# The samples' last 16 steps of gathered rows: from the stage of the weighted sums to behind the first half's last norm

## The chip, the cores and the metric

The kernel runs on one core of one Trainium2 chip. The metric is device time in microseconds (us) of one execution, the median over several runs. The profile is one execution on the same core, read by the hardware profiler. The engines are PE (TensorE, with PEld for its weight loads), DVE (VectorE), ACT (ScalarE), POOL (GpSimd) and SP (SyncE). Each takes its own instructions strictly in order.

## What is computed

One layer of a hybrid decoder for 512 prompt tokens and 32 sample tokens (8 sequences of 4), 544 columns in all, 1024 channels. Two token mixers come first; the change doesn't touch them. Then come a product-key expert layer and a gate, and the change lies where these two meet:

```python
def peer_ffn(h, ...):                # per token: 8 heads, 16 of 16384 experts each
    ...
    act = gelu(einsum('nd,nhkd->nhk', hb, expert_u[idx]))
    wgt = gate * act
    return einsum('nhk,nhkd->nd', wgt, expert_v[idx])

x = x + peer_ffn(rmsnorm(x, g_ffn), ...)
ple_gate = sigmoid(rmsnorm(x, g_ple) @ w_ple_gate)
x = x + (p @ w_ple) * ple_gate       # y = rmsnorm(x, g_final)
```

## The kernel before

**Tokens.** The first 384 prompt tokens (ND) go through the experts densely: all 16384 experts are computed in 128 blocks, masked by gates. The other 128 prompt tokens and the 32 sample tokens use gathered rows: a step is either a dot of a gathered row of expert_u with the token (`dot`, lines 1115 to 1117) or a gathered row of expert_v times its weight, added to an accumulator (`add`, lines 1122 to 1127). The prompt's 128 tokens have one token per partition and 128 picks, 256 steps. The 32 samples are laid four times over the 128 partitions, a quarter of the heads each, so 32 picks and 64 steps. `sides` hands out these 320 steps in order; the last 16 are adds of picks 16 to 31 of the samples. In front of the first of them stands one small product (line 1137) of 16 weights with their gates. The accumulators are `accs[0]` (prompt) and `accs[1]` (samples; the trace calls the tile accg).

**A gather** (line 1109) is an indirect DMA on POOL's queue of 128 rows of 1024 floats, 512 KB, into one of four buffers `rows` (NGR). A buffer is free again when the dot or add that read it is done.

**The stage of the weighted sums** (loop over j at line 1204 on) multiplies the 128 blocks' activations with expert_v on PE into three accumulators `pacc`, 36 matmuls of 512 columns for a block. The weights are float32 split in two parts: ACT copies the high part (line 123, whi), DVE subtracts to get the low part (line 124, wlo); three products stand for one. The loop takes three of the 320 steps per block. What is left is written out behind it (lines 1214, 1215). A scheduler places the instructions on each engine, so DVE's order isn't the order of the text.

**The last stage** begins with pacc: for three blocks of 128 tokens ACT copies pacc into `ot`, PE transposes it (line 1250), DVE adds it to x (line 1252, `residual`). Beside this the PLE input p is multiplied with w_ple on PE (line 1266, pw). Then the 544 columns are treated as two halves of 272 columns (HS). Half 0, the first half, holds prompt tokens only, all of them dense. Half 1, the second, holds the rest: dense tokens, the 128 tokens of accs[0] (`residual(3, ...)`) and the 32 samples, which a product with `sel` folds from four copies to one (line 1287, pts). The loop at lines 1277 to 1297 makes for each half the norm (`rms_rstd`: squares on ACT, line 98 and 101; sums sa on DVE, line 102; a product with ones; root on ACT with its table load, line 108; broadcast on PE, line 116), scales x (xn, line 1295) and splits it into fh and fl. The second loop, lines 1298 to 1314, makes for each half 8 chunks: a weight block of 512 KB is loaded and split, PE does 24 matmuls of 272 columns (line 1304, pj), ACT the sigmoid (sg, line 1306), DVE multiplies by pw and adds to x (lines 1307, 1308). Then come the final norm, its scaling (yo, line 1313) and the stores. The text calls the chunks 0 to 7 (half 0) and 8 to 15 (half 1). High and low parts of a weight block have two buffers, so the split for chunk c+2 waits for PE's end of chunk c.

`tc.issue_after(ins)` binds the instructions that are written in its block, those on the engine of `ins` alone, to come behind `ins` on that engine.

Of the kernel before, what the change touches and what calls it, by code (L numbers as in the profile page):

```python
# [14 lines left out]
OP = mybir.AluOpType  # L15
# [27 lines left out]
LATE = 110  # L43
XL, NYO = 118, 6
TW = 3, 2
NXN = 3
NRW, NHW = 3, 4
BACT = (4, 4, 4)
# [8 lines left out]
def step_kernel(ctx: ExitStack, tc: tile.TileContext, xT, pT, pk, wab, win, wbr, wout, wq, keysT, eu, eur, ev,  # L57
                wple, wpg, sh, sd, scv, yT, o_hp, o_dp, o_cv, o_hs, o_ds, gdram, ysp, gsp, x1s, asp, usp):
    nc = tc.nc
    V, S, G, PE = nc.vector, nc.scalar, nc.gpsimd, nc.tensor  # L60
# [9 lines left out]
    def par(name, i=0, n=1):  # L70
        return pkt[:, PK[name] + i:PK[name] + i + n]
# [50 lines left out]
    def split(hi, lo, src):  # L122
        S.activation(hi, src, AF.Copy)  # L123
        return V.tensor_sub(lo, src, hi.bitcast(F32))  # L124
# [3 lines left out]
    def wload(src, blocks=True):  # L128

        raw = wr.tile([128, 1024], F32, name="wraw", tag="wraw", bufs=NRAW)  # L130
        nc.sync.dma_start(raw, src)
        hi = wp.tile([128, 1024], F32R, name="whi", tag="whi", bufs=NHI)
        lo = wp.tile([128, 1024], F32R, name="wlo", tag="wlo", bufs=NHI)
        split(hi, lo, raw)
        if not blocks:
            return hi, lo
        return hi.rearrange("p (k c) -> p k c", c=128), lo.rearrange("p (k c) -> p k c", c=128)
# [55 lines left out]
    for hf in range(2):  # L193
        r0 = rms_rstd(sp_, pn0, lambda k: x0[:, k, HS[hf]], 8, hf)
        for k in range(8):
            xn = sp_.tile([128, HT], F32, name="xn", tag="xn", bufs=3)
# [580 lines left out]
    for h in range(NH):  # L777
# [4 lines left out]
        i = done = 0  # L782
# [90 lines left out]
    for i, hi, lo in ((0, hh, hl), (1, hh2, hl2)):  # L873
        if i:
            r1 = rms_rstd(x1p, pn1, lambda k: x1[:, k, HS[1]], 8, 1)
        for k in range(8):
            xn = hf[:, k] if i else qp.tile([128, HT], F32, name="xn", tag="xn", bufs=2)
# [106 lines left out]
    def ublock(j):  # L984
        ps = dots_u(*wload(eu[j]))
        i = slots.pop(0)
        acts[j] = act[:, i], i
        S.activation(act[:, i], ps[:, :ND], AF.Gelu_apprx_tanh)
# [152 lines left out]
    def sides():  # L1141
        yield from g_steps(0, htok, 128)
        yield from g_steps(1, hsam, 32)

    steps = sides()
    made = 0
# [21 lines left out]
    def prep(j):  # L1168

        wh = ep.tile([128, ND], F32R, name="wgh", tag="wgh", bufs=2)  # L1170
        wl = ep.tile([128, ND], F32R, name="wgl", tag="wgl", bufs=2)
        raw = wr.tile([128, 1024], F32, name="vraw", tag="wraw", bufs=NRAW)
        loads.append(nc.sync.dma_start(raw, ev[j]))
        if j >= NPRE and j % 4 == 0:
            ggs[0] = ggs.pop(j, None) or gates_in()
            nc.sync.dma_start(ggs[0], gdram[:, (j - NPRE) // 4])
        if j + 3 in spilled:
            reload(j + 3)
        a, i = acts.pop(j)
        if j >= NPRE:  # L1180
            V.tensor_mul(a.rearrange("p (c n) -> p c n", n=32), a.rearrange("p (c n) -> p c n", n=32), ggs[0][:, :, j % 4])
        gated.append(split(wh, wl, a))
        if i is not None:
            slots.append(i)
        vh = wp.tile([128, 1024], F32R, name="whi", tag="whi", bufs=NHI)
        vl = wp.tile([128, 1024], F32R, name="wlo", tag="wlo", bufs=NHI)
        split(vh, vl, raw)
        return wh, wl, vh, vl

    def products(j, wh, wl, vh, vl):  # L1190
        for i, (w_, v_) in enumerate(((wh, vh), (wl, vh), (wh, vl))):
            for t in range(3):
                ts = slice(t * 128, (t + 1) * 128)
                for hf in range(2):
                    PE.matmul(pacc[t][:, hf], w_[:, ts], v_[:, hf * 512:(hf + 1) * 512],  # L1195
                              start=(j == 0 and i == 0), stop=(j == 127 and i == 2))
# [6 lines left out]
    for j in range(128):  # L1203
        now = ready
        while late and len(acts_made) < nlate * (j + 1) / LATE:
            acts_made.append(late.pop(0))
            ublock(acts_made[-1])
        if j < 127:
            ready = prep(j + 1)
        products(j, *now)  # L1210
        with tc.issue_after(gated[min(HJ, j + 1)].ins) if j < HOLD else ExitStack():
            for _ in range(3):
                next(steps, None)
    for _ in steps:
        pass
    eps.close()
    wst.close()
    lts.close()
# [12 lines left out]
    def tile_(tag, bufs, shape, dt=F32):  # L1231
        return lp.tile(shape, dt, name=tag, tag=tag, bufs=bufs)

    yo0 = [tile_("yo", NYO, [128, 2, HT]) for _ in range(2)]
    tile_("xn3", NXN, [128, HT])
    tile_("sg2", 2, [128, HT])
    ph = tile_("fh", 2, [128, 2, T], F32R)
    pl = tile_("fl", 2, [128, 2, T], F32R)
    NRAW, NHI = TW
    wp = wr = tail.enter_context(tc.tile_pool(name="wpt", bufs=2, side="right", reuse_waits="tile"))  # L1240
# [6 lines left out]
    def residual(t, ot, k0):  # L1247
        p = psu.tile([128, 512], F32, name="pt", tag="pu").rearrange("p (a b) -> p a b", a=4)
        for k in range(4):
            PE.transpose(p[:, k], ot[:, k * 128:(k + 1) * 128], ident)  # L1250
        xc = x1[:, k0:k0 + 4, t * 128:(t + 1) * 128]
        V.tensor_add(xc, xc, p)
# [20 lines left out]
    def norm(i):  # L1273
        xs = x1[:, :, HS[i]]
        r = rms_rstd(x2p, pn.tile([128, 512], F32, name="pn", tag="pn").rearrange("p (a b) -> p a b", a=1),
                     lambda k: xs[:, k], 8, 0)
        return xs, r

    parts = []
    for i in range(2):  # L1280
        if i == 1:
            for k0 in range(0, 8, 4):
                residual(3, accs[0][:, k0 * 128:k0 * 128 + 512], k0)
            for k0 in range(0, 8, 4):
                p = psu.tile([128, 512], F32, name="pts", tag="pu")[:, :4 * NS].rearrange("p (a b) -> p a b", a=4)
                for k in range(4):
                    PE.matmul(p[:, k], accs[1][:, (k0 + k) * 128:(k0 + k + 1) * 128], sel, start=True, stop=True)
                xc = x1[:, k0:k0 + 4, TP:]
                V.tensor_add(xc, xc, p)
        xs, r2 = norm(i)  # L1290
        hh = tile_("fh", 2, [128, 8, HT], F32R)
        hl = tile_("fl", 2, [128, 8, HT], F32R)
        for k in range(8):
            xn = tile_("xn3", NXN, [128, HT])
            V.scalar_tensor_tensor(xn, xs[:, k], par("g_ple", k), r2, op0=OP.mult, op1=OP.mult)
            split(hh[:, k], hl[:, k], xn)
        parts.append((hh, hl))
    for i, (hh, hl) in enumerate(parts):
        for c in range(8):
            wh, wl = wload(wpg[c])  # L1300
            ps = psj.tile([128, 512], F32, name="pj", tag="pj")[:, :HT]
            for k in range(8):
                for j, (a, b) in enumerate(((wh, hh), (wh, hl), (wl, hh))):
                    PE.matmul(ps, a[:, k], b[:, k], start=(k == 0 and j == 0), stop=(k == 7 and j == 2))  # L1304
            sg = tile_("sg2", 2, [128, HT])
            S.activation(sg, ps, AF.Sigmoid)
            V.tensor_mul(sg, sg, pw[:, c, HS[i]])
            V.tensor_add(x1[:, c, HS[i]], x1[:, c, HS[i]], sg)
        xs, r3 = norm(i)
        for k in range(0, 8, 2):  # L1310
            yo = tile_("yo", NYO, [128, 2, HT])
            for m in range(2):
                V.scalar_tensor_tensor(yo[:, m], xs[:, k + m], par("g_final", k + m), r3, op0=OP.mult, op1=OP.mult)
            nc.sync.dma_start(yT[:, k:k + 2, HS[i]], yo)
# [86 lines left out]
```

## Time and profile before

| what | value |
|---|---|
| runs: median (lowest to highest) | 2048.83 us (2047.22 to 2049.85), 3 runs |
| the profiled execution, its own time | 2056.58 us |
| its span, first to last instruction | 2054.8 us |
| mean granted clock of TensorE in it | 0.979 |
| PE busy | 1976.8 us, 96% |
| DVE busy | 1703.0 us, 83% |
| ACT busy | 1032.8 us, 50% |
| POOL busy | 506.5 us, 25% |

The profiled execution is 7.75 us longer than the median. A share of busy time is an average over stages with different limits: what a change in one stage is worth has to be read from that stage's windows, and from what each engine's idle time there ended on. Times below are microseconds from the start of the span.

### The profile page before, as it was taken

How to read it: one execution, taken by the hardware profiler on the slowest of the kernel's cores; microseconds unless marked ns; L12 is line 12 of the kernel's file. 1: busy time of each engine (PE TensorE's matmuls, PEld its weight loads, DVE VectorE, ACT ScalarE, POOL GpSimd, SP SyncE). 2: the span in 40 equal slices, each digit the busy share in tenths (PEclk: the TensorE clock that was granted, in tenths of full speed). 3: DMA queues.
4: the chain of work that ended last, by engine and by line, in shares of the span. 5: the costliest groups of instructions: out<-in, count | busy, mean ns of one | idle time of the engine just before them, and what ended most of it. 6: DMA issues, size and time to landing. Idle time of an engine off the chain costs nothing.

```text
span 2054.8 us, 34654 instructions
## 1 busy us (share of the span) xinstructions
PE 1976.8 (96%) x12292; PEld 1833.8 (89%) x12292; DVE 1703.0 (83%) x4579; ACT 1032.8 (50%) x1720; POOL 506.5 (25%) x509
## 2 busy tenths in 40 slices
PE   6999999999998999999999999999999999999887
PEld 6899888988998999999999888888888888888677
DVE  7677988876566799999999788888887888887887
ACT  5657576663534446765666433333333333333354
POOL 0001010000100001213332255544343344344510
PEclk9999999989999999999999999999999999999979
DMA  4324443444755238999999899999999999989843
GB/s 163 117 98 139 153 161 120 161 145 171 267 195 190 76 97 201 253 263 346 391 370 351 294 358 343 339 352 336 341 342 352 336 341 341 359 314 338 303 161 126
DMA packets 189421, 518.86 MB, mean 253 GB/s; under 512 B 18609, under 2 KB 72241, under 8 KB 189121
## 3 DMA queue, kind: packets, MB, share of 16 engines
q1 hardware_dynamic: 132384, 311.70, 43.5%
q0 software_dynamic: 56864, 204.96, 29.6%
q8 instruction: 96, 1.57, 0.3%
q14 instruction: 77, 0.62, 0.1%
HBM read 455.80 MB, written 60.79 MB: 251 GB/s over the span
## 4 chain that ended last, share of the span: by engine, by line
PE 83%; DVE 5%; DMA 5%; issue 4%; ACT 2%; POOL 1%; SPq 0%; DVEq 0%; POOLq 0%; ACTq 0%
PE pacc L1195 21%; PE pj L166 15%; PE pu L968 8%; PE pu L967 8%; PE pu L970 8%; PE pj L917 5%; PE pg L1084 4%; PE pj L1304 2%; DMA rows<-in_ev,idxs 2%; PE pmb L554 1%; POOL rows L1109 1%; PE pma L349 1%; PE pmb L545 1%; DMA usp<-lraw 1%; DMA lraw<-in_eu 1%
## 5 line engine op out<-in xcount | busy, mean ns | idle before, releaser
L967 PE MATMUL pu<-hh,whi 128*128 128x384 f32 x1024 | 346.2, 338 | 2.6 <-ACT act L978 2.6
L968 PE MATMUL pu<-hl,whi 128*128 128x384 f32 x1024 | 345.8, 338 | 0.0
L1109 POOL DMA_INDIRECT rows<-in_ev,idxs x160 | 208.6, 1304 | 275.3 <-DVE accg L1127 245.1
L124 DVE TENSOR_TENSOR wlo<-wraw,whi 128x1024 fp32r<-128x1024 f32 x169 | 206.2, 1220 | 79.9 <-ACT whi L123 71.4
L1109 POOL DMA_INDIRECT rows<-in_eur,idxs x160 | 199.7, 1248 | 250.6 <-DVE jk L1117 208.4
L123 ACT ACTIVATE whi<-wraw 128x1024 fp32r<-128x1024 f32 x169 | 178.5, 1057 | 159.9 <-PE pj L166 84.5
L1127 DVE SCALAR_TENSOR_TENSOR accg<-rows,wts,accg 128x1024 f32<-128x1024 f32 x158 | 202.2, 1279 | 9.5 <-DMA rows<-in_ev,idxs 9.0
L970 PE MATMUL pu<-hh,wlo 128*128 128x384 f32 x1024 | 202.2, 336 | 0.0
L1195 PE MATMUL pacc<-whi,wgl 128*128 128x512 f32 x768 | 197.1, 392 | 3.2 <-DVE wgl L124 3.2
L967 PEld LDWEIGHTS pu<-hh,whi 128*128 128x128 f32 x1024 | 192.7, 188 | 6.1 <-ACT act L978 3.6
L1195 PE MATMUL pacc<-whi,wgh 128*128 128x512 f32 x768 | 196.9, 391 | 0.2 <-ACT wgh L123 0.2
L1195 PE MATMUL pacc<-wlo,wgh 128*128 128x512 f32 x768 | 196.5, 391 | 0.0
L123 ACT ACTIVATE whi<-vraw 128x1024 fp32r<-128x1024 f32 x128 | 135.0, 1055 | 119.6 <-PE pacc L1195 85.0
L968 PEld LDWEIGHTS pu<-hl,whi 128*128 128x128 f32 x1024 | 192.6, 188 | 2.5
L124 DVE TENSOR_TENSOR wlo<-vraw,whi 128x1024 fp32r<-128x1024 f32 x128 | 156.6, 1223 | 43.0 <-ACT whi L123 38.0
L166 PE MATMUL pj<-xh,whi 128*128 128x272 f32 x768 | 175.4, 302 | 3.8 <-ACT sg L692 2.5
L970 PEld LDWEIGHTS pu<-hh,wlo 128*128 128x128 f32 x1024 | 178.6, 188 | 0.0
L1195 PEld LDWEIGHTS pacc<-whi,wgl 128*128 128x128 f32 x768 | 144.8, 189 | 35.3 <-DVE wgl L124 4.0
L166 PE MATMUL pj<-xh,wlo 128*128 128x272 f32 x768 | 174.5, 301 | 0.6 <-DVE wlo L124 0.6
L166 PE MATMUL pj<-xl,whi 128*128 128x272 f32 x768 | 173.4, 300 | 0.2 <-DVE xl L124 0.2
L1195 PEld LDWEIGHTS pacc<-wlo,wgh 128*128 128x128 f32 x768 | 145.0, 189 | 30.2
L1195 PEld LDWEIGHTS pacc<-whi,wgh 128*128 128x128 f32 x768 | 143.2, 188 | 26.9 <-ACT wgh L123 0.5
(488 smaller groups left out, 4312.1 us busy)
## 6 DMA issues: line engine op xcount, KB each, us to landing
wraw<-in_eu SPq DMA_DIRECT2D x128, 512.0 KB, 6.3
vraw<-in_ev SPq DMA_DIRECT2D x128, 512.0 KB, 6.6
wraw<-in_win SPq DMA_DIRECT2D x48, 512.0 KB, 3.7
gg<-gdram SPq DMA_DIRECT2D x25, 768.0 KB, 7.4
gdram<-go SPq DMA_DIRECT2D x36, 512.0 KB, 10.1
lraw<-in_eu SPq DMA_DIRECT2D x34, 512.0 KB, 4.2
usp<-lraw SPq DMA_DIRECT2D x34, 512.0 KB, 2.6
wlo<-usp SPq DMA_DIRECT2D x34, 512.0 KB, 8.1
```

The lines of the kernel that those rows point to most:

```text
L123: S.activation(hi, src, AF.Copy)
L124: return V.tensor_sub(lo, src, hi.bitcast(F32))
L166: PE.matmul(ps[:, hf, :HT], a, b[:, HS[hf]], start=(i == 0 and j == 0), stop=(i == n - 1 and j == 2))
L917: PE.matmul(p[:, i, :HT], w_[:, k], x_[:, k, :HT], start=(k == 0 and j == 0), stop=(k == 7 and j == 2))
L967: PE.matmul(ps[:, :ND], wh[:, k], hh[:, k], start=(k == 0), stop=False)
L968: PE.matmul(ps[:, :ND], wh[:, k], hl[:, k], start=False, stop=False)
L970: PE.matmul(ps[:, :ND], wl[:, k], hh[:, k], start=False, stop=(k == 7))
L1084: PE.matmul(p[:, j], A[:, j], B[:, j], start=True, stop=True)
L1109: G.indirect_dma_start(out=r, out_offset=None, in_=src, in_offset=bass.IndirectOffsetOnAxis(ap=idx, axis=0))
L1127: V.scalar_tensor_tensor(accs[i], r, wts[i][:, k:k + 1], accs[i], op0=OP.mult, op1=OP.add)
L1195: PE.matmul(pacc[t][:, hf], w_[:, ts], v_[:, hf * 512:(hf + 1) * 512], start=(j == 0 and i == 0), stop=(j == 127 and i == 2))
L1304: PE.matmul(ps, a[:, k], b[:, k], start=(k == 0 and j == 0), stop=(k == 7 and j == 2))
```

## The change

The loop over the blocks now stops handing out steps at 304 of the 320 (HELD = 16). The last 16, the samples' adds of picks 16 to 31 with their gathers and the product of 16 weights, are written behind half 0's scalings, and their DVE instructions are bound to come behind the last of these scalings. Lines of the changed file are 1 higher up to half 0's scalings and 5 higher behind them.

```diff
--- before.py
+++ after.py
@@ -43,6 +43,7 @@
 LATE = 110
 XL, NYO = 118, 6
 TW = 3, 2
+HELD = 16
 NXN = 3
 NRW, NHW = 3, 4
 BACT = (4, 4, 4)
@@ -1210,9 +1211,9 @@
         products(j, *now)
         with tc.issue_after(gated[min(HJ, j + 1)].ins) if j < HOLD else ExitStack():
             for _ in range(3):
-                next(steps, None)
-    for _ in steps:
-        pass
+                if made < 320 - HELD:
+                    next(steps)
+                    made += 1
     eps.close()
     wst.close()
     lts.close()
@@ -1292,9 +1293,13 @@
         hl = tile_("fl", 2, [128, 8, HT], F32R)
         for k in range(8):
             xn = tile_("xn3", NXN, [128, HT])
-            V.scalar_tensor_tensor(xn, xs[:, k], par("g_ple", k), r2, op0=OP.mult, op1=OP.mult)
+            scaled = V.scalar_tensor_tensor(xn, xs[:, k], par("g_ple", k), r2, op0=OP.mult, op1=OP.mult)
             split(hh[:, k], hl[:, k], xn)
         parts.append((hh, hl))
+        if i == 0:
+            with tc.issue_after(scaled.ins):
+                for _ in steps:
+                    pass
     for i, (hh, hl) in enumerate(parts):
         for c in range(8):
             wh, wl = wload(wpg[c])
```

**DVE between the sums and half 0's scaling.** `accg` is the samples' accumulator, `x_13925` the residual, `sel`, `pt` and `wlo`, `fl` as above. Before, from the copies to sel on:

```order
L1228 COPY sel<-ident 32x32 x4
L1127 SCALAR_TENSOR_TENSOR accg_6858<-rows,wts_6856,accg_6858 128x1024
L1252 TENSOR_TENSOR x_13925<-x_13925,pt 128x4x128 x2
L1127 SCALAR_TENSOR_TENSOR accg_6858<-rows,wts_6856,accg_6858 128x1024
L1252 TENSOR_TENSOR x_13925<-x_13925,pt 128x4x128 x2
L1127 SCALAR_TENSOR_TENSOR accg_6858<-rows,wts_6856,accg_6858 128x1024
L124 TENSOR_TENSOR wlo<-wraw,whi 128x1024
L1252 TENSOR_TENSOR x_13925<-x_13925,pt 128x4x128 x2
L124 TENSOR_TENSOR wlo<-wraw,whi 128x1024
L1127 SCALAR_TENSOR_TENSOR accg_6858<-rows,wts_6856,accg_6858 128x1024
```

And with the change, from the last add that stays:

```order
L1128 SCALAR_TENSOR_TENSOR accg_6858<-rows,wts_6856,accg_6858 128x1024
L1229 COPY sel<-ident 32x32 x4
L1253 TENSOR_TENSOR x_13925<-x_13925,pt 128x4x128 x6
L125 TENSOR_TENSOR wlo<-wraw,whi 128x1024 x2
L103 TENSOR_TENSOR sa<-sa,sq 128x272
L125 TENSOR_TENSOR fl<-yo,fh 128x544 x2
L103 TENSOR_TENSOR sa<-sa,sq 128x272 x6
L108 TENSOR_SCALAR rs<-pn 128x3
```

The adds to accg that stood between the adds to x, the splits and the sums are gone from here; the six adds to x are neighbours, and so are the sums sa.

**DVE in half 0's chunks.** Each chunk has a split wlo (of a later chunk), a product with pw (sg) and an add to x. Before, three chunks in, with half 1's norm between:

```order
L1308 TENSOR_TENSOR x_13925<-x_13925,sg_21291 128x272
L1295 SCALAR_TENSOR_TENSOR xn_21135<-x_13925,pkt,pn 128x272
L124 TENSOR_TENSOR wlo<-wraw,whi 128x1024
L1295 SCALAR_TENSOR_TENSOR xn_21139<-x_13925,pkt,pn 128x272
L1307 TENSOR_TENSOR sg_21326<-sg_21326,pw 128x272
L1295 SCALAR_TENSOR_TENSOR xn_21143<-x_13925,pkt,pn 128x272
L102 TENSOR_TENSOR sa<-sa,sq 128x272
L124 TENSOR_TENSOR fl<-xn_21135,fh 128x272
L124 TENSOR_TENSOR wlo<-wraw,whi 128x1024
L1307 TENSOR_TENSOR sg_21361<-sg_21361,pw 128x272
L1308 TENSOR_TENSOR x_13925<-x_13925,sg_21326 128x272
```

With the change, the last two chunks of half 0 and what follows:

```order
L1312 TENSOR_TENSOR sg_21396<-sg_21396,pw 128x272
L1128 SCALAR_TENSOR_TENSOR accg_6858<-rows,wts_6856,accg_6858 128x1024
L1313 TENSOR_TENSOR x_13925<-x_13925,sg_21396 128x272
L125 TENSOR_TENSOR wlo<-wraw,whi 128x1024
L1312 TENSOR_TENSOR sg_21431<-sg_21431,pw 128x272
L1128 SCALAR_TENSOR_TENSOR accg_6858<-rows,wts_6856,accg_6858 128x1024
L1313 TENSOR_TENSOR x_13925<-x_13925,sg_21431 128x272
L1128 SCALAR_TENSOR_TENSOR accg_6858<-rows,wts_6856,accg_6858 128x1024 x4
L1290 TENSOR_TENSOR x_13925<-x_13925,pts 128x4x32
L103 TENSOR_TENSOR sa<-sa,sq 128x272 x2
L1290 TENSOR_TENSOR x_13925<-x_13925,pts 128x4x32
L103 TENSOR_TENSOR sa<-sa,sq 128x272 x8
```

Half 1's scalings, splits and sums have left the chunks. One held add stands in each chunk, four stand behind the last, and half 1's sums come only behind these.

**ACT behind chunk 7's sigmoid** (`sg_21431`). Before:

```order
L1306 ACTIVATE sg_21396<-pj 128x272
L101 ACTIVATE sq<-x_13925 128x272
L123 ACTIVATE fh<-xn_21147 128x272
L101 ACTIVATE sq<-x_13925 128x272
L123 ACTIVATE whi<-wraw 128x1024
L1306 ACTIVATE sg_21431<-pj 128x272
L123 ACTIVATE fh<-xn_21151 128x272
L101 ACTIVATE sq<-x_13925 128x272 x2
L123 ACTIVATE whi<-wraw 128x1024
L1306 ACTIVATE sg_21520<-pj 128x272
```

With the change:

```order
L124 ACTIVATE whi<-wraw 128x1024
L1311 ACTIVATE sg_21431<-pj 128x272
L99 ACTIVATE sa<-x_13925 128x272
L102 ACTIVATE sq<-x_13925 128x272 x2
L99 ACTIVATE sa<-x_13925 128x272
L102 ACTIVATE sq<-x_13925 128x272 x10
L109 ACT_TABLE_LOAD
L109 ACTIVATE rs<-rs 128x3
L102 ACTIVATE sq<-x_13925 128x272 x2
L109 ACTIVATE rs<-rs 128x3
L124 ACTIVATE fh<-xn_21123 128x272
```

Squares (sa, sq), root and splits fh of half 1 were spread over half 0's chunks, up to the sigmoid of chunk 7 here. Now they all stand behind it, with the squares of half 0's final norm among them, and in front of the first sigmoid of half 1 (sg_21520). The order of POOL's gathers is the same in both kernels. On SP the loads of the last three of the 16 weight blocks come behind half 0's four stores now, in front of them before.

## Rows read from the trace of the kernel before

**Rows 1.** The page: busy time by engine; GB/s in 40 equal slices.
```profile
PE 1976.8 (96%) x12292; PEld 1833.8 (89%) x12292; DVE 1703.0 (83%) x4579; ACT 1032.8 (50%) x1720; POOL 506.5 (25%) x509
...
GB/s 163 117 98 139 153 161 120 161 145 171 267 195 190 76 97 201 253 263 346 391 370 351 294 358 343 339 352 336 341 342 352 336 341 341 359 314 338 303 161 126
```

**Rows 2.** Windows: length, then PE, PEld, DVE, ACT, POOL busy (count), clock, DMA share, GB/s.
```profile
1200.00:1830.00 630.00, 630.00 (x3075) 559.28 (x3074) 525.34 (x660) 229.02 (x309) 272.69 (x214) 1.00 0.94 343
1941.00:1956.00 15.00, 5.27 (x26) 4.20 (x25) 11.65 (x16) 5.51 (x10) 8.27 (x6) 0.67 0.96 351
1956.00:1979.00 23.00, 19.18 (x131) 17.72 (x130) 21.15 (x33) 13.12 (x32) 6.86 (x5) 0.85 0.61 212
1979.00:2014.00 35.00, 31.77 (x215) 30.79 (x215) 28.74 (x67) 24.70 (x48) 0.00 (x0) 0.85 0.30 102
2014.00:2042.00 28.00, 25.72 (x198) 24.75 (x196) 22.97 (x50) 15.84 (x28) 0.00 (x0) 1.00 0.42 134
```

**Rows 3.** The chain that ended last, 1937 to the end: start, us, what.
```profile
1944.61 9.61 DMA rows<-in_ev,idxs
...
1954.86 1.28 DVE x L1252 x2
...
1978.44 1.31 DVE xn L1295 x3
...
2041.58 0.41 ACT sg L1306
...
2047.87 0.50 DVE yo L1313
```

**Rows 4.** Groups by line, DVE, 1937 to 1976: busy, mean ns, idle before, releaser.
```profile
L1127 DVE SCALAR_TENSOR_TENSOR accg<-rows,wts,accg 128x1024 f32<-128x1024 f32 x16 | 20.5, 1282 | 5.9 <-DMA rows<-in_ev,idxs 5.6
...
L124 DVE TENSOR_TENSOR fl<-yo,fh 128x544 fp32r<-128x544 f32 x2 | 1.4, 716 | 0.0
```

**Rows 5.** Timeline, DVE: start, length, line, operation, count.
```profile
1964.30 2.08 DVE L102 TENSOR_TENSOR sa<-sa,sq 128x272 f32<-128x272 f32 x4
...
2001.95 1.22 DVE L124 TENSOR_TENSOR wlo<-wraw,whi 128x1024 fp32r<-128x1024 f32 x1
...
2003.09 0.43 DVE L1307 TENSOR_TENSOR sg<-sg,pw 128x272 f32<-128x272 f32 x1
...
2003.79 1.14 DVE L124 TENSOR_TENSOR fl<-xn,fh 128x272 fp32r<-128x272 f32 x3
...
2028.16 3.35 DVE L1313 SCALAR_TENSOR_TENSOR yo<-x,pkt,pn 128x272 f32<-128x272 f32 x8
...
2043.48 0.44 DVE L102 TENSOR_TENSOR sa<-sa,sq 128x272 f32<-128x272 f32 x1 [0.55 <-ACT sq L101]
```

**Rows 6.** Timeline, SP; and transfers by line: KB, median us to landing.
```profile
1941.19 0.80 SPq L131 DMA_DIRECT2D wraw<-in_wple  x2
...
wraw<-in_wple SPq DMA_DIRECT2D x2, 512.0 KB, 5.3
```

**Rows 7.** Timeline, PE, 1962 to 1964.
```profile
1962.21 0.43 PE L1266 MATMUL pw<-fl,whi 128*128 128x272 f32 x1
1962.44 0.43 PE L1266 MATMUL pw<-fh,wlo 128*128 128x272 f32 x1
...
1963.21 0.29 PE L1266 MATMUL pw<-fh,whi 128*128 128x272 f32 x1
1963.33 0.29 PE L1266 MATMUL pw<-fl,whi 128*128 128x272 f32 x1
```

**Rows 8.** Timeline, ACT: the sigmoids of chunks 7 and 9.
```profile
2013.87 0.38 ACT L1306 ACTIVATE sg<-pj 128x272 f32<-128x272 f32 x1
...
2021.11 0.39 ACT L1306 ACTIVATE sg<-pj 128x272 f32<-128x272 f32 x1
```

**Rows 9.** The tile rows, 1937 to 1976: its gathers.
```profile
DMA to landing us min/median/max: 4.3/5.9/9.6
```

## The prediction

> **What bounds the kernel now.** I read the page's busy line first: PE is busy 96% of the span [rows 1], so outside the tail a microsecond of DVE or POOL is worth little. The windows by stage [rows 2] say where that stops. In the stage of the weighted sums PE has no gap. From 1941 to 1956 it is busy 5.27 of 15 us and DVE 11.65; from 1956 to 1979 DVE is busy 21.15 of 23; from there to the end PE leads again. The chain that ended last [rows 3] shows who decides in that trough: a gather's landing for 9.61 us, DVE's adds to x, and at 1978.44 the first scaling xn of the first half. From then on it is the gate's matmuls until the sigmoid at 2041.58, and a fixed end of norm, scaling and stores.
>
> The trough is where the moved work lies. Of DVE's groups from 1937 to 1976 [rows 4] the 16 adds of the samples' last 16 rows take 20.5 us, with 5.9 us of idle before them, 5.6 of it for rows that hadn't landed. DVE takes its queue in order, so residual adds and the norm's sums stand behind rows in flight.
>
> **The change, step by step.** It moves 16 gathers, 16 adds and one product of 16 weights; it adds and removes none. Times are of the profiled execution, whose last sigmoid is at 2041.58. In what follows a DVE instruction costs its length less 0.08, since the next starts that much before its end (a split at 2001.95 of 1.22, the next at 2003.09) [rows 5].
>
> *Step 1, the first half's scaling comes earlier.* PE's end of the sums (1941) doesn't move, as nothing there waits for these adds. The three residual rounds no longer stand behind rows: at 1.3 us of adds each [rows 3], plus some 0.3 for evacuation and transposes, they end near 1946. Then the PLE weights are late next: issued at 1941.19, landing 5.3 us later [rows 6], so 1946.5. Two splits (2.3), two 544-column splits (1.3, [rows 4]) and seven sums at 0.52 (four in 2.08 [rows 5]; 3.6) give 1953.7. From the last sum to the first scaling the final norm took 2043.92 to 2047.87, 3.95 us [rows 3, 5]; with 0.8 for PE, which now has PLE products between, xn starts at 1958.5. That is **20 us earlier**. POOL's order is unchanged: the first four held gathers still go out as buffers come free, before 1940, and wait in their buffers; the other twelve each wait for an add.
>
> *Step 2, the first half's eight chunks.* From 1958.5 DVE has 8 scalings (0.41 each by the three in 1.31 [rows 3]; 3.3), 8 splits (0.35 each by the three in 1.14 [rows 5]; 2.8), chunk 0's weights (1.1), the 16 weights (0.1), three held adds (3.6), one add to x (0.6) and chunk 1's weights (1.1): 12.6, so 1971.1. Here the held adds are on the path: chunk 1 can't pass its third matmul before. Then each chunk costs DVE a split, a product, a held add and an add to x: 1.14 + 0.35 + 1.20 + 0.35 = 3.04. PE's 24 matmuls of 272 columns start 0.12 to 0.13 apart at the full clock [rows 7]; at 0.126 they are 3.03. The two are level, so the held adds hide here, with nothing to spare. Chunk 1 ends at 1974.4 and chunk 7 at 1992.7. Before, chunk 7's sigmoid was at 2013.87 [rows 8]: still 20 us ahead.
>
> *Step 3, the hole.* Behind chunk 7's weights (ready 3 us before its end) DVE has three products, adds and x adds and two more splits, 8.0 us: 1997.7. Then the last four adds, 4.8: 2002.5. The last row can be later: its buffer comes free four adds earlier, near 1997.4, and gathers land 4.3 to 9.6 us after issue, 5.9 in the middle [rows 9]. At 5.9 the last add runs 2003.3 to 2004.5; I take 2004.3. The sample rows' product with sel (0.8) and the add (0.3) give 2005.4. ACT's order now puts the squares of both halves behind chunk 7's sigmoid: ten sums until the second half's own is complete, at 0.52, make 5.2. The root needs its table (1.28, hidden behind the last chunk before), and then the 3.95 from sum to scaling: 2015.8, first matmul 2016.7. PE, which was fed through this point before, is empty for **24 us**.
>
> *Step 4, restart.* Chunks 8 and 9 advance with DVE's 8 scalings, 8 splits and the first half's 8 output scalings (3.35 [rows 5]), 9.4: 2025.2. The last 12 matmuls behind that, at the 0.227 apart of [rows 7], take 2.7: 2027.9, where chunk 9's sigmoid was at 2021.11 [rows 8]. The six chunks left took 20.5 from there to 2041.58. I add 0.7, since chunks 8 and 9 now end together and both next weights wait for them. The last sigmoid comes at 2049.1, **7.5 us late**. Norm, stores and end are unchanged.
>
> As a check: 20 gained, 24 lost in the hole, some 3.5 lost by two norms and the output scalings in front of chunks 8 and 9.
>
> Free edits: the table loads in the gate fall from five to three, 1.28 each, but ACT is 24.7 of 35 us busy there [rows 2], so zero; if ACT were late they would be worth 2 us. The loop that stops at 304 steps issues nothing new. On SP the last three weight blocks now come behind half 0's stores; they are for chunks 13 to 15, over 15 us later, so zero, and if a store held one up its chunk would wait for what is left of the 5.3 us of a landing [rows 6].
>
> The clock: through the trough the granted clock is 0.67 in the mean [rows 2], and PE's 272-column matmuls are still 0.23 apart at 1962.21, the level of 1.2 GHz, and 0.12 apart at 1963.21, that of 2.4 GHz [rows 7]. The new hole is longer than the gaps ahead of that, so chunks 8 and 9 should start at 1.2 GHz. They are paced by DVE, so I charge only the 12 last matmuls.
> The Trainium skill ("TensorE: Matmul & The Clock Gate", Part 1) says that an idle array falls back to half rate and that only activity releases it. That speaks against opening a hole in front of 8 chunks. By it a start that stops and goes at DVE's pace could stay at half rate into chunk 10, 24 x 0.1 = 2.4 us more, 2058.7; the row at 1962.21 agrees, since PE had worked in pieces before it and was still slow. By the pace alone it is the 2056.3 below.
>
> **The rivals.**
>
> *A, faster: the hole is shorter than the lead.* If DVE's list keeps up with PE, so that the last add ends 1 us ahead of chunk 7's end instead of 11.6 behind it, all that follows comes 12.6 us earlier than in the sum: a hole of 11.4, and the end 5.1 before the old one, 2043.7. It breaks even at a last add near 1996.8. For it: four rows stand ready and POOL idles. Against: DVE needs 3.04 a chunk beside PE's 3.03, four adds stand behind the last chunk, and ACT's order puts no square before its sigmoid. 0.05.
>
> *B, no change: lead and hole cancel.* Rows land in 4.3, xn starts 1.5 us sooner since fewer gathers share the engines with the PLE weights, and the restart costs 1.5 less: +2 to +4, so 2051 to 2052.9. 0.12.
>
> *C, slower still: the transfers bind the first half.* Each chunk now carries a 512 KB weight block and a 512 KB gather, 1.05 MB in 3.04 us, 345 GB/s; that is what the core moved through the sums, 343 GB/s over 630 us at a DMA share of 0.94 [rows 2], where the old gate asked for 102. At the sums' lower slices (314 GB/s in the page [rows 1]) a chunk is 0.3 longer, 2.4 in eight; a last row at 9.6 adds 3.7. Together 2059 to 2064. 0.15.
> The Trainium skill ("DMA: Bandwidth & Descriptors", Bandwidth) puts transfers of 1 MB at 341 GB/s and the ceiling above 420; by its ceiling C costs nothing, by its figure for 1 MB it sits on the edge, where the row is.
>
> *D, the change doesn't do what it says.* The order ties only DVE's adds to the scaling. Had it held POOL too, the first rows would land 5.9 after 1966 and chunk 1 would wait some 5 us: 2061. The order of POOL speaks against it. 0.03.
>
> **The numbers.** The forecast has 0.65: 2048.83 + 7.5, **2056.3**, with its own 2053 to 2059. The sum is against one profiled execution of 2056.58, 7.8 above the median of the runs shown; I move the difference to the median, since the tail's parts don't depend on what slowed that execution earlier. The known ends: low, landing 4.3 (-0.7), step 1 early (-1.5), restart (-1.5): +3.8. High: landing 9.6 (+3.7), transfers (+2.4), step 1 late by 1.5: +15. The range 2051 to 2064 leaves out A and half of the far ends. A difference of 0.2%, 4.1 us, is about what a measurement of this kernel can tell from none. Faster 0.05 (A), the same 0.12 (B), slower 0.83.
>
> **What would show it.** After the change: the first xn near 1958; six adds to x in a row on DVE behind the copies to sel; chunk 7's sigmoid near 1994; a PE hole of over 20 us behind it, with the last four adds, the sample product and 14 sums inside; the first sg of the second half past 2025. If the hole is under 16 us, or xn doesn't come 15 us sooner, the sum is wrong; if the chunks of the first half take 3.4 us or more with DVE waiting for rows, it is C.

## The result, and the profile after

| | before | after | forecast |
|---|---|---|---|
| runs in one comparison: median (lowest to highest) | 2049.85 us (2047.22 to 2056.07), 5 runs | 2065.39 us (2063.34 to 2073.35), 5 runs | 2056.3, range 2051 to 2064 |
| ratio, with its 95% interval | 1 | 1.0063 (1.0036 to 1.0089) | 1.0037 |
| span of the profiled execution | 2054.8 us | 2061.4 us | |

The change is slower, by about 13 us with the ratio (7 to 18); the two medians lie 15.5 us apart. The forecast had the sign and the mechanism. Its size was short: the ratio on the median of 2048.83 that it started from is 2061.7, inside the range, while the median of the five runs is 1.4 us above its upper end.

The two profiled executions differ already ahead of the tail: PE's last matmul of the weighted sums ends at 1941.16 before and at 1936.49 after. In the 14 profiled executions of this study that end lies between 1925.9 and 1942.2. Most of this spread is there at the first matmul of the sums (1142.1 to 1157.4), far ahead of the 16 steps that the edits move. From here on times of a tail are counted from **the end of the sums**, and the **tail** is the time from there to the end of the span.

| from the end of the sums, us | before | forecast | after |
|---|---|---|---|
| first scaling of the first half | 37.3 | 17.3 | 18.0 |
| chunk 7's sigmoid | 72.7 | about 52 | 54.6 |
| last add | 33.4 | 63.1 | 64.5 |
| first scaling of the second half | 59.6 | 74.6 | 79.2 |
| last sigmoid | 100.4 | 107.9 | 111.7 |
| tail | 113.6 | 121.1 | 124.9 |

So the tail grew by 11.3 us where the forecast had 7.5. The page still shows nothing of it, against [rows 1] the busy line reads the same:

```profile
PE 1974.0 (96%) x12292; PEld 1830.9 (89%) x12292; DVE 1705.4 (83%) x4579; ACT 1029.4 (50%) x1718; POOL 511.8 (25%) x509
```

The windows by stage of after, in the columns of [rows 2] (window, its length, busy time and count of PE, PEld, DVE, ACT and POOL, granted clock, DMA share, GB/s): up to the first scaling, the first half, the hole, chunks 8 and 9, the rest to the last sigmoid.

```profile
1936.50:1954.50 18.00, 13.42 (x79) 11.48 (x78) 11.49 (x23) 12.42 (x26) 0.00 (x0) 0.81 0.52 178
1954.50:1990.30 35.80, 33.90 (x254) 32.19 (x253) 34.42 (x51) 18.72 (x35) 12.28 (x10) 1.00 0.71 243
1990.30:2016.70 26.40, 7.83 (x35) 7.53 (x35) 19.15 (x41) 9.50 (x23) 1.89 (x2) 0.58 0.31 109
2016.70:2027.30 10.60, 9.65 (x54) 9.07 (x54) 8.61 (x24) 3.90 (x9) 0.00 (x0) 0.76 0.31 105
2027.30:2048.60 21.30, 18.70 (x144) 18.25 (x144) 14.93 (x26) 11.70 (x21) 0.00 (x0) 1.00 0.23 75
```

The third row is the hole and the change's price: in 26.4 us PE is busy 7.83, with small products and at a granted clock of 0.58, while DVE works 19.15. In the first half, the second row, both are nearly full (33.90 and 34.42 of 35.80). The chain that ended last (start, length, what; to be held against [rows 3]) goes through the same places:

```profile
1954.51 1.31 DVE xn L1296 x3
...
1995.14 4.48 DMA rows<-in_ev,idxs
...
2015.64 1.31 DVE xn L1296 x3
...
2027.28 1.28 ACT L1311
...
2028.97 0.95 ACT whi L124
...
2029.97 18.19 PE pj L1309 x142
```

Before, it hung on a gather's landing ahead of 1978.44. Now such a landing stands behind chunk 7, and behind it two norms. DVE in the order of time (start, length, engine, line, operation, output and inputs, count; in brackets the idle time before it and what ended it), with the rows that answer to [rows 4, 5]:

```profile
1936.97 1.28 DVE L1253 TENSOR_TENSOR x<-x,pt 128x512 f32<-128x512 f32 x2 [5.31 <-PE pt L1251]
1938.47 1.29 DVE L1253 TENSOR_TENSOR x<-x,pt 128x512 f32<-128x512 f32 x2 [0.21 <-PE pt L1251]
1939.97 1.29 DVE L1253 TENSOR_TENSOR x<-x,pt 128x512 f32<-128x512 f32 x2 [0.21 <-PE pt L1251]
...
1976.72 1.23 DVE L125 TENSOR_TENSOR wlo<-wraw,whi 128x1024 fp32r<-128x1024 f32 x1 [1.28 <-ACT whi L124]
...
1979.77 1.26 DVE L125 TENSOR_TENSOR wlo<-wraw,whi 128x1024 fp32r<-128x1024 f32 x1
...
1982.84 1.25 DVE L125 TENSOR_TENSOR wlo<-wraw,whi 128x1024 fp32r<-128x1024 f32 x1
...
1999.71 1.28 DVE L1128 SCALAR_TENSOR_TENSOR accg<-rows,wts,accg 128x1024 f32<-128x1024 f32 x1 [0.65 <-DMA rows<-in_ev,idxs]
2003.07 0.29 DVE L1290 TENSOR_TENSOR x<-x,pts 128x128 f32<-128x128 f32 x1 [2.07 <-PE pts L1288]
...
2005.92 3.56 DVE L103 TENSOR_TENSOR sa<-sa,sq 128x272 f32<-128x272 f32 x7 [0.21 <-ACT sq L102]
```

The six adds to x are neighbours, as forecast. One chunk is 3.07 (1979.77 to 1982.84). At 1976.72 DVE had waited for ACT, which had waited for a weight block. The last add ends at 2000.99, the first add of the samples' product comes 2.07 later, and from 2005.92 on the sums of both norms go by in one row. ACT and PE in the same form; the sigmoids answer to [rows 8], the matmuls to [rows 7]:

```profile
1991.13 0.38 ACT L1311 ACTIVATE sg<-pj 128x272 f32<-128x272 f32 x1
2003.39 0.43 ACT L99 ACTIVATE sa<-x 128x272 f32<-128x272 f32 x1 [11.88 <-DVE x L1290]
...
2009.96 1.28 ACT L109 ACT_TABLE_LOAD   x1
...
2028.57 0.40 ACT L1311 ACTIVATE sg<-pj 128x272 f32<-128x272 f32 x1
...
2048.18 0.40 ACT L1311 ACTIVATE sg<-pj 128x272 f32<-128x272 f32 x1 [1.15 <-PE pj L1309]
```

```profile
2001.14 3.59 PE L1288 MATMUL pts<-sel,accg 128*128 128x32 f32 x16 [10.88 <-DVE accg L1128]
...
2008.05 1.44 PE L105 MATMUL pn<-ones,sa 128*128 128x1 f32 x6 [3.31 <-DVE sa L103]
2012.85 1.44 PE L105 MATMUL pn<-ones,sa 128*128 128x1 f32 x6 [3.37 <-DVE sa L103]
2014.16 1.44 PE L117 MATMUL pn<-ident,rs 128*128 128x128 f32 x6
...
2016.65 0.82 PE L1309 MATMUL pj<-fh,whi 128*128 128x272 f32 x2 [1.05 <-ACT fh L124]
...
2029.97 0.39 PE L1309 MATMUL pj<-fh,whi 128*128 128x272 f32 x1 [2.13 <-ACT whi L124]
2030.20 0.29 PE L1309 MATMUL pj<-fl,whi 128*128 128x272 f32 x1
2030.32 0.29 PE L1309 MATMUL pj<-fh,wlo 128*128 128x272 f32 x1
```

ACT is idle for 11.88 us behind chunk 7's sigmoid and takes the root's table at 2009.96 in the middle of the squares. PE has the second half's seven sums at 2008.05, but its broadcast L117, which frees the scalings, comes at 2014.16, behind the product of the first half's sums at 2012.85. The gate's matmuls start again at 2016.65. And POOL, the gathers of [rows 9]: the first one in 31 us waits for the first held add (1961.70 to 1962.98), since four held rows had been fetched ahead, as forecast.

```profile
1963.25 0.94 POOL L1110 DMA_INDIRECT rows<-in_ev,idxs  x1 [31.05 <-DVE accg L1128]
```

### The profile page after: what moved, and what is told of

It is laid out like the page before. It is cut to its first block, busy times and chain, and to the rows that moved or that the text cites. A ratio compares the mean times of both kernels' runs of the same rounds, so it can differ in the third digit from the quotient of the medians.

```text
span 2061.4 us, 34659 instructions
## 1 busy us (share of the span) xinstructions
PE 1974.0 (96%) x12292; PEld 1830.9 (89%) x12292; DVE 1705.4 (83%) x4579; ACT 1029.4 (50%) x1718; POOL 511.8 (25%) x509
## 4 chain that ended last, share of the span: by engine, by line
PE 84%; DVE 6%; DMA 4%; ACT 3%; issue 2%; POOL 0%; SPq 0%; DVEq 0%; POOLq 0%; ACTq 0%
PE pacc L1196 25%; PE pj L167 13%; PE pu L969 9%; PE pu L968 9%; PE pu L971 9%; PE pj L918 5%; PE pg L1085 4%; DMA lraw<-in_eu 2%; DMA usp<-lraw 1%; PE pj L1309 1%; PE pmb L555 1%; PE pmb L546 1%; PE pma L350 1%; DVE wlo L125 1%; PE psc L939 1%
## 5 line engine op out<-in xcount | busy, mean ns | idle before, releaser
L1128 DVE SCALAR_TENSOR_TENSOR accg<-rows,wts,accg 128x1024 f32<-128x1024 f32 x158 | 202.3, 1280 | 11.3 <-DMA rows<-in_ev,idxs 10.8
```

The lines of the kernel that those rows point to most:

```text
L1128: V.scalar_tensor_tensor(accs[i], r, wts[i][:, k:k + 1], accs[i], op0=OP.mult, op1=OP.add)
```

## The experiments

All tails, counted as above. The ratio is to the kernel before, on the same chip in the same comparison.

| run | first scaling | last add | second half's scaling | last sigmoid | tail | ratio (95%) |
|---|---|---|---|---|---|---|
| before | 37.3 | 33.4 | 59.6 | 100.4 | 113.6 | 1 |
| after | 18.0 | 64.5 | 79.2 | 111.7 | 124.9 | 1.0063 (1.0036 to 1.0089) |
| e1 no held adds | 18.1 | none | 51.7 | 87.0 | 100.6 | 0.9956 (0.9935 to 0.9976) |
| e2 adds only | 18.2 | 62.5 | 77.1 | 109.7 | 122.8 | 1.0057 (1.0033 to 1.0081) |
| e3 late final norm | 17.1 | 63.2 | 74.7 | 110.6 | 127.0 | 1.0061 (1.0043 to 1.0078) |
| e4 HELD = 8 | 27.6 | 54.2 | 74.3 | 108.3 | 121.5 | 1.0036 (1.0018 to 1.0053) |
| e5 behind the residual | 37.0 | 39.5 | 59.2 | 100.0 | 113.1 | 1.0002 (0.9986 to 1.0018) |
| e6 HELD = 4 | 30.2 | 43.7 | 65.5 | 101.0 | 114.2 | 1.0005 (0.9987 to 1.0023) |
| e7 eight adds on POOL | 33.6 | 48.7 | 78.6 | 114.0 | 127.7 | 1.0081 (1.0052 to 1.0110) |
| e8 sixteen on POOL | 31.0 | 62.7 | 88.6 | 122.6 | 135.8 | 1.0133 (1.0108 to 1.0159) |
| e9 final norm behind the scalings | 19.1 | 64.5 | 75.9 | 111.9 | 125.0 | 1.0084 (1.0056 to 1.0112) |
| e10 e5 and e9 together | 35.6 | 38.1 | 56.4 | 95.9 | 109.3 | 1.0003 (0.9986 to 1.0020) |
| e11 before, again | 36.5 | 32.5 | 59.1 | 99.9 | 113.1 | one run, no ratio |
| e12 e10, again | 38.4 | 40.9 | 59.6 | 99.1 | 112.3 | 0.9987 (0.9964 to 1.0009) |

**e1: the held adds left out.** From the changed kernel:

```diff
-        if i == 0:
-            with tc.issue_after(scaled.ins):
-                for _ in steps:
-                    pass
```

> Left out: the samples' last 16 gathers, their 16 adds and the product of their 16 weights (the sums of the samples miss these picks). Counted from the end of the weighted sums' last matmul, the tail took 113.6 us before and 124.9 after. Theory (the held adds alone make the hole, the lead is real): first scaling at +18 us as after the change, no PE gap over 4 us in front of the second half, last sigmoid some 63 us behind the first scaling as before the change; tail 94 to 97 us, so some 17 to 20 us under the kernel before. Rival (the hole is made by the order, the squares of both halves behind chunk 7, whatever the adds do): a gap of 12 us or more stays in front of the second half and the tail is 106 us or more.

Measured: tail 100.6, between the two. The lead is real, and without the adds the hole is nearly gone: chunk 8's sigmoid comes 10.6 us behind chunk 7's, 37.5 in the change and 6.0 before. But of 19.2 us of lead at the first scaling only 13.0 reach the end (9.0 by the ratio, 4.9 to 13.3). The windows show where the rest goes:

```profile
1990.00:1996.00 6.00, 5.51 (x44) 5.25 (x43) 5.51 (x14) 4.92 (x11) 0.00 (x0) 1.00 0.38 105
1996.00:2002.00 6.00, 4.79 (x34) 4.15 (x34) 6.00 (x16) 2.85 (x8) 0.00 (x0) 1.00 0.44 158
2002.00:2008.00 6.00, 3.77 (x29) 3.33 (x29) 4.19 (x14) 5.59 (x8) 0.00 (x0) 1.00 0.11 20
```

Around the seam between the halves DVE is busy 6.00 of 6 us and PE 4.79: the second half's scalings and splits and the first half's own norm all stand there. The chain that ended last runs through DVE, nearly without a break, from 1990.75 to 1999.80. By these tails the 16 adds with their gathers cost 13.0 us where they stood (113.6 less 100.6) and 24.3 where the change puts them (124.9 less 100.6).

**e2: the adds without their gathers.**

```diff
-            r = gather(ev.rearrange("j a d -> (j a) d"), idxs[:, 2 * i + 1, k:k + 1])
+            if not held[0]:
+                last[0] = gather(ev.rearrange("j a d -> (j a) d"), idxs[:, 2 * i + 1, k:k + 1])
+            r = last[0]
...
         if i == 0:
+            held[0] = True
```

> The 16 held adds stay where the change puts them, but read the row that was gathered last instead of gathering rows of their own (the samples' sums get that row 16 times): 16 gathers, 8 MB, are gone. Theory (DVE's queue sets the first half and the hole): the 1.3 us wait for a weight block and the 0.65 us wait for the last row go, no more; the tail falls from 124.9 to 122 to 123.5 us, the hole in front of the second half stays over 22 us. Rival (the transfers bind the first half): chunks of under 3.0 us, and 5 us or more off the tail.

Measured: the tail fell by 2.1 to 122.8, the last add by 2.0; a chunk is 3.04. The line of the transfers in 25 us of the first half, after the change and then without the held gathers:

```profile
DMA packets 2231, 8.18 MB, mean 327 GB/s; under 512 B 241, under 2 KB 241, under 8 KB 2228
```

```profile
DMA packets 1151, 4.22 MB, mean 169 GB/s; under 512 B 125, under 2 KB 125, under 8 KB 1149
```

Half of the traffic gone changes almost nothing. The 2.1 us are the two waits that the theory named, 1.3 for a weight block and 0.65 for the last row; the rest is DVE's.

**e3 and e9: the first half's final norm out of the hole.** e3 binds it behind chunk 9 on DVE and ACT, e9 some 6 us earlier, behind the second half's last split on DVE (`cut`) and its last rounding on ACT (`seen`):

```diff
+        with tc.issue_after(seen.ins), tc.issue_after(cut.ins):
             xs, r3 = norm(i)
             ...
```

> Held adds as in the change; the first half's final norm and output scalings are bound behind chunk 9 on DVE and ACT. Theory (the hole behind the last add holds two norms in turn, and the restart stands behind eight output scalings): seven sums (3.6 us) leave the stretch from the last add to the second half's first scaling, so 14.6 us become 10 to 11.5, and chunks 8 and 9 end 2 to 3.5 us sooner after it; the tail falls from 124.9 to 117 to 120 us, some of it given back at the end by the late outputs. Rival (only the held adds count): under 2 us off.

> Held adds as in the change; the first half's final norm (squares, sums, root, output scalings) is bound behind the second half's last split on DVE and its last rounding on ACT, that is some 6 us earlier than behind chunk 9. Theory (the step that was mis-sized is the stretch behind the last add: the first half's squares and root run inside it): last add to second scaling 11 to 12 us where the change has 14.6, chunks 8 and 9 two to four us sooner behind it; unlike the run with the norm behind chunk 9 nothing is pushed to the end, so tail 118 to 121 us against 124.9. Rival (what leaves the hole comes back in the second half, at half clock or on ACT's tables): tail 123 or more.

Measured: the first part of both theories came as said, from the last add to the second half's scaling 11.5 us in both where the change has 14.6. The second part fell: tails 127.0 and 125.0. In e3 the first 27 matmuls behind a pause of 2.13 in front of chunk 10 were 0.23 apart, at a granted clock of 0.50 (1.2 GHz), where those of the change behind the same pause at 2029.97 were 0.12 apart, at 1.00 (2.4 GHz); and the eight output scalings stand in front of the last sums:

```profile
2019.64 0.60 PE L1317 MATMUL pj<-fh,whi 128*128 128x272 f32 x1 [2.13 <-ACT whi L124]
2020.03 0.43 PE L1317 MATMUL pj<-fl,whi 128*128 128x272 f32 x1
2020.26 0.43 PE L1317 MATMUL pj<-fh,wlo 128*128 128x272 f32 x1
```

```profile
2044.09 3.35 DVE L1308 SCALAR_TENSOR_TENSOR yo<-x,pkt,pn 128x272 f32<-128x272 f32 x8
```

In e9 the first 15 matmuls behind that pause were as slow, two more table loads of ACT stand between the sigmoids of chunks 10 and 11, and the same eight scalings stand in front of a weight split:

```profile
2027.94 1.28 ACT L109 ACT_TABLE_LOAD   x1
...
2031.42 1.28 ACT L1314 ACT_TABLE_LOAD   x1
```

```profile
2033.98 3.35 DVE L1322 SCALAR_TENSOR_TENSOR yo<-x,pkt,pn 128x272 f32<-128x272 f32 x8
```

From the last add to the last sigmoid it is 47.2 us in the change, 47.4 in e3 and 47.5 in e9. So none of the three places behind the last add is cheaper, but not for one reason: at 0.10 us for each slow matmul 2.7 us of e3's stretch and 1.5 of e9's are the clock.

**e4 and e6: fewer held adds**, HELD = 8 and 4.

> HELD = 8 in place of 16. Theory (lead and hole are two prices on DVE): the first scaling comes 1 to 3 us later than with 16, since four of the eight adds that go back stand between the residual rounds; the last held add ends some 9.6 us sooner (8 adds of 1.2) and some of the second half's squares are done by chunk 7, so the hole shrinks from 26 us to 12 to 16 us; tail 111 to 116 us, level with the kernel before. Rival (each add put back delays the first scaling by the 1.25 us that the 16 cost together): the first scaling 10 us later, the tail unchanged near 124.

> HELD = 4. Theory (each add put back stands between the residual rounds behind rows in flight): first scaling 30 to 34 us after the sums' end, last held add near 46, tail 113 to 117 us, level with the kernel before. Rival (four adds are hidden in the first half's chunks and lead without a hole): tail under 110 us.

Measured: with 8 the first scaling is 9.6 us later than with 16, as the rival said, yet the tail falls by 3.4. The last add comes 10.3 us sooner and the second half's scaling only 4.9: now chunk 7 and not the last add stands in front of it (chunk 7's sigmoid at 64.5, the scaling 9.8 later, with the first half's own norm between). With 4 the first scaling is 7.1 us sooner than in the kernel before and the second half's 5.9 later, and the tail is the same. Why e4's first scaling is late shows in its chain and on DVE: one gather took 9.82 us, and residual adds stood behind its add.

```profile
1929.17 9.82 DMA rows<-in_ev,idxs
```

```profile
1934.76 1.28 DVE L1128 SCALAR_TENSOR_TENSOR accg<-rows,wts,accg 128x1024 f32<-128x1024 f32 x1 [3.38 <-DMA rows<-in_ev,idxs]
```

**e5: all 16 behind the last residual add** instead of behind the scalings.

```diff
-        V.tensor_add(xc, xc, p)
+        return V.tensor_add(xc, xc, p)
...
-            residual(t, ot, k0)
+            done = residual(t, ot, k0)
+    with tc.issue_after(done.ins):
+        for _ in range(16):
+            next(steps, None)
```

> All 16 held steps are issued behind the last of the six residual adds instead of behind the first half's scalings. Theory (DVE's tail queue is one sum of work: what counts is that the adds neither stand in front of the residual rounds nor behind the first half's chunks): the first scaling comes 33 to 36 us after the sums' end (37.3 before, 18.0 after the change), the second half's scalings 54 to 59 us after it and so inside the first half's chunks, no hole; tail 107 to 112 us, 2 to 6 us under the kernel before and 13 to 17 under the change. Rival (rows in flight block the norm's sums as before, one for one): first scaling at 37 or later, tail 113 to 116.

Measured: the rival; first scaling 37.0, tail 113.1. The residual adds run at once, but now each sum of the norm waits behind an add (1953.06, 1954.25), and once for a row in flight:

```profile
1939.04 1.28 DVE L1253 TENSOR_TENSOR x<-x,pt 128x512 f32<-128x512 f32 x2 [5.31 <-PE pt L1251]
...
1953.06 1.28 DVE L1128 SCALAR_TENSOR_TENSOR accg<-rows,wts,accg 128x1024 f32<-128x1024 f32 x1
1954.25 0.43 DVE L103 TENSOR_TENSOR sa<-sa,sq 128x272 f32<-128x272 f32 x1
...
1968.12 1.28 DVE L1128 SCALAR_TENSOR_TENSOR accg<-rows,wts,accg 128x1024 f32<-128x1024 f32 x1 [2.65 <-DMA rows<-in_ev,idxs]
```

**e7 and e8: the adds on other engines.** From the kernel before, the last 8 adds (in e8 all 16):

```diff
-            if k == 0:
+            if i == 1 and k >= nk - 8:
+                S.activation(r, r, AF.Copy, scale=wts[i][:, k:k + 1])
+                G.tensor_add(accs[i], accs[i], r)
+            elif k == 0:
```

> From the kernel before: the last 8 of the 16 adds leave DVE; ACT scales the landed row by its weight in place and POOL adds it to the sums. Theory (the tail is bound by DVE's sum of work; adds that run beside it need neither stand in front of the residual rounds nor behind the chunks): first scaling 26 to 31 us after the sums' end as with HELD = 8, no hole over 5 us in front of the second half, since POOL ends the eight adds before chunk 5; tail 103 to 109 us, so 5 to 10 us under the kernel before. Rival (POOL's adds hold up DVE's instructions one for one, or POOL takes over 3 us for one): DVE's 1024-column instructions grow by 0.3 us or more beside them or the last add comes after chunk 6, and the tail is 113 us or more.

> As the run before with all 16 adds on POOL. Theory: first scaling at 18 to 20 us as after the change, and the second half's norm waits for POOL's last add instead of DVE's: at some 2 us for one add and a row each 4 us behind the last free buffer, 16 adds end 40 to 50 us after the sums' end, a hole of 5 to 12 us in front of the second half; tail 106 to 113 us. Rival (POOL and DVE hold each other up): tail over 118 us.

Measured: the rivals, tails 127.7 and 135.8. POOL needs 2.38 us for an add, DVE 1.28, and while POOL adds, DVE's sums stand:

```profile
1952.46 4.90 POOL L1126 TENSOR_TENSOR accg<-accg,rows 128x1024 f32<-128x1024 f32 x2
...
1958.50 2.38 POOL L1126 TENSOR_TENSOR accg<-accg,rows 128x1024 f32<-128x1024 f32 x1
```

```profile
1951.20 0.97 DVE L102 TENSOR_TENSOR sa<-sa,sq 128x272 f32<-128x272 f32 x2
1952.51 8.68 DVE L102 TENSOR_TENSOR sa<-sa,sq 128x272 f32<-128x272 f32 x4 [0.33 <-ACT sq L101]
```

Four sums of 0.43 take 8.68 us, against 0.97 for the two ahead of them. ACT's scalings of the rows stand in its queue too; how much of the two tails is theirs was not tried apart.

**e10 to e12: e5 and e9 together, and how firm a tail is.**

> All 16 held steps behind the last residual add (as in the run behind the residual, tail 113.1) and the first half's final norm behind the second half's last split. Theory (with the second half's norm done inside the first half's chunks, the first half's own norm is what still stands in front of chunks 8 and 9, 5 to 6 us between the sigmoids of chunks 7 and 8): chunk 8 follows chunk 7 in 3 to 4 us, tail 107 to 111 us, under the kernel before by 3 to 6. Rival (DVE's work only changes its place and comes back in chunks 9 to 14): tail 112 to 115, no difference from the kernel before.

> The kernel before, unchanged, for a second profiled execution: the tails of all runs are compared with the one of 113.6 us. If the tail is a fixed cost that does not depend on the weighted sums ahead of it: 113 to 114.5 us whatever the span. If the rows' landing times move it from execution to execution: off by 2 us or more, and then differences of tails under that size say nothing.

> The kernel with all held steps behind the last residual add and the first half's final norm behind the second half's last split, a second profiled execution. Fixed tail: 108.5 to 110 us again, 4 us under the kernel before, and the comparison of times (1.0003, from 0.9986 to 1.0020) has the difference of the stretches ahead of the tail in it. Rival: 111 us or more, so that the first one was a lucky landing of rows.

Measured: the kernel before repeats its tail within 0.5 us (113.6, 113.1). The combination had 109.3 and then 112.3; its times against before are 1.0003 and 0.9987. Its first profile looked like a gain of 4.3 us, the second one like 1.4. What differs between these two is the first scaling (35.6 and 38.4), which still waits for rows. Behind it the gain repeats: from the first scaling to the last sigmoid it is 60.3 and 60.7 us, against 63.1 and 63.4 in the kernel before and 63.1 in e5. These 2.7 us are 0.13% of the kernel, inside both intervals, so the times neither show nor exclude them. In both, chunk 8 follows chunk 7 within 3.2 us as the theory said (6.0 before), but half of that comes back by the end, where the eight output scalings stand in front of a weight split:

```profile
2026.19 3.35 DVE L1325 SCALAR_TENSOR_TENSOR yo<-x,pkt,pn 128x272 f32<-128x272 f32 x8
2029.46 1.22 DVE L127 TENSOR_TENSOR wlo<-wraw,whi 128x1024 fp32r<-128x1024 f32 x1
```

No version that computes everything was measured to beat the kernel before.

## Why the prediction came out as it did

*Step 1, right.* 20 us forecast, 19.3 measured at the first scaling. The sums ended 0.4 us sooner than in the forecast, and the way from the last sum to the scaling took 5.9 where 4.75 was taken.

*Step 2, right in its pace, 2.3 us late at its end.* 3.04 forecast for a chunk, 3.07 measured. PE's last matmul of chunk 7 ends at 53.8 from the sums' end, 51.5 forecast: 0.7 from step 1, 1.3 of DVE's wait at 1976.72 for a weight block, which the sum didn't have. That is rival C in small: e2 prices all of the gathers at 2.1 us, not at the 2.4 and 3.7 that C had on top of the sum.

*Step 3, the term that was mis-sized.* The last add came 1.4 us late (64.5 for 63.1); its row landed in 4.48 us where 5.9 was taken, which gave some of step 2 back. Behind it, "two norms" were priced too low: from the last add to the second half's scaling 14.65 us instead of 11.5. Of this 1.3 lies in the samples' product, which ran at a granted clock of 0.50 (2.4 with its add, 1.1 forecast). The second half's own sums were not late: its seven are complete 4.6 behind that add, 5.2 forecast. The miss is the way from there to the scaling, 7.6 instead of 5.2 (1.28 and 3.95). On it the product of the sums takes 1.44 at the slow clock (0.81 in the norm behind chunk 15 of the kernel before), two sums of the first half stand between its steps on DVE (2011.81 and 2012.36), and its broadcast waits on PE for the product of the first half's sums. e3 and e9, without the first half's norm there, have the same product of 2.4 and the same sums, and 4.5 for this way.

*Step 4, close, by two errors that cancel.* 33.3 us forecast from that scaling to the last sigmoid, 32.5 measured. Chunk 9's sigmoid came 14.2 behind the scaling, 12.1 forecast: the chain there goes through ACT, with a table load of 1.28 and a weight copy of 0.95 that the sum didn't have. The six chunks left took 18.4 instead of 21.2, for the 20.5 that was taken from before held the first half's norm products and a split at 2031.42 behind the eight output scalings [rows 5], and the sum had charged these scalings in front of chunk 9 already. So 7.5 + 1.4 for the last add + 3.2 - 0.8 = 11.3, the tail's growth.

*What it missed.* The check at the end of the sum spoke of 20 us gained. e1 shows that without any hole only 13.0 would have come out at the end; its windows and its chain put the rest on DVE, which is full at the seam of the halves. The forecast had these microseconds only as "3.5 lost" in front of chunks 8 and 9. No dose and no place of the 16 adds alone that was tried changed the tail for the better: e4 to e6 move work within one nearly full queue.

*The rivals.* A needed a hole of 11.4 us; it is 26.4. Of B's conditions the landing nearly came (4.48 for 4.3), but the scaling was 0.7 late and not 1.5 early. C is worth 2.1 us. D didn't happen: four rows were fetched ahead. The restart at half clock that was set at 2058.7 didn't reach chunk 10 in the change (0.12 apart at 2030.20); it did in e3 and e9, for 27 and 15 matmuls, where that text had 24. The low end of the sum put a landing of 4.3 at -0.7; with the sum's own times (1997.4, 4.3 and an add of 1.2 against 2004.3) it is -1.4, which bears on nothing, since the result lies on the other side.

*The base.* The sum was moved from the profiled execution to the median. The spread of the sums' end, 16 us over 14 executions, is larger than the effect, so a single time of each says little; the five times of each in the comparison don't overlap.

## What to carry to other kernels

Before moving work off a path, add up the engine that does it over the whole stretch to the end: DVE was nearly full in the second part of the trough (21.15 of 23 us) and full at the seam, so the same adds cost 13 us in one place and 24 in the other, and no place tried in between was free. An add that waits behind another stage's work delays whatever is normalised or summed from it; ask for the next consumer, and whether the bounding engine has work until then. And compare tails from a common event, with a second profile of each kernel, before believing 4 us.

## What the runs showed of the hardware that was not expected

**POOL holds up DVE.** In e7 a sum of two SBUF tiles that takes 0.43 us took 2.66, 2.41 and 2.89 beside POOL's adds of 2.38, and 0.45 at 1957.76, between two of these adds. The scaling xn, which reads one operand from PSUM, kept its 0.49 us beside them. The Trainium skill ("SBUF — State Buffer", Who interferes with whom) says that a DVE instruction with two SBUF inputs contends with a POOL instruction that reads SBUF for a shared port, and that this is an exclusive lock. The trace agrees for DVE; POOL's adds kept about 2.4 us, so no wait on their side shows.

**The same pause, two clocks.** Behind a pause of PE of 2.13 us (2.14 in e9) in front of chunk 10 the granted clock was 1.00, that is 2.4 GHz, after the change (2029.9 to 2034.0). In e3 it was 0.50, that is 1.2 GHz, from 2019.6 to 2025.7, and in e9 0.54 from 2021.8 to 2025.3. In all three a pause of 0.77 and two matmuls stand ahead of it, and PE had come up to 2.4 GHz only during chunks 8 and 9: at 2021.7 in the change, 8.2 us ahead of chunk 10, and some 7 us ahead of it in the other two. What decides between the two levels these runs don't settle.
